# Early fill products, another order in the first conditioning steps, paired sums of squares and a later bias preparation in a decoder block on one core

## The chip, the cores and the metric

The kernel runs on one core of one Trainium2 chip. Its time is that of one execution on the device in microseconds (us); the median of several executions counts. The engines are TensorE (PE, with its weight loads as PEld), VectorE (DVE), ScalarE (ACT), GpSimd (POOL) and SyncE (SP), whose queue issues nearly all loads. TensorE has two clock levels, 1.2 and 2.4 GHz; the profile gives the granted clock as a share of the upper one.

## What is computed

One decoder block on 256 tokens of width 1024: a conditioned norm, one wide input product, a convolution branch and a gated linear recurrence branch (8 heads), their gated merge through three square products, then a mixture of 32 experts of which each token takes four, and a last norm.

```python
mod = silu(c) @ w_ada + b_ada                    # six sections of 1024
sh1, sc1, ga1, sh2, sc2, ga2 = split(mod, 6)
h = rmsnorm(x, g_mix) * (1 + sc1) + sh1
p = h @ w_in                                     # 8 parts of 1024 columns
y_conv = silu(layernorm(conv31(p_a * sigmoid(p_b)))) @ w_conv_out
y_hg   = (rmsnorm_head(hgrn2(p_q, p_f, p_i, lb)) * silu(p_g)) @ w_hgrn_out
x = x + ga1 * ((sigmoid(p_gc) * y_conv + sigmoid(p_gh) * y_hg) @ w_out)
h2 = rmsnorm(x, g_ffn) * (1 + sc2) + sh2
x = x + ga2 * moe(h2)      # top 4 of 32, clamped SwiGLU, w1[e] 1024x2048, w2[e] 1024x1024
out = rmsnorm(x, g_final)
```

## The kernel before, in words

**Slots and loads.** All weights, and the large intermediates, live in 22 slots of 1 MiB. `queue` lists the loads in the order of use, `load` issues the next one on SP's queue, and `free` gives a slot back and calls `pump`, which issues as many loads as the list `LOADS` says for that release: 19 at the start (line 42), then 0 to 3 for each release. From the experts on, `pump` loads whenever a slot is free. Small tiles come from a pool of eight buffers (`temp`), and products go to eight PSUM banks (`bank`).

**Products in two parts.** Weights and activations are split into a rounded part and a rest, both float32r. `split_half(n, i)` (from line 359) does it for half of weight block n: ScalarE casts (line 370), VectorE or GpSimd subtracts (line 372; the lists `SPLIT_DVE` and `SPLIT_HALF` say which). `prod_kt` (line 386) issues three matmuls for each 128 rows and 128 columns, so a block of 1024 by 256 has 48. `block_product(n)` splits block n + 1 while it multiplies block n. Float32 products that aren't split are issued as two MATMUL instructions each.

**First steps.** Lines 228 to 304 and the loop over `st` are in a hand-written order on PE, ACT and DVE. The square of x (line 232) and the sigmoid of c (line 234) come first, then the sum of squares over the rows by `column_parts` and `column_total` (lines 243 to 252), the reciprocal root (lines 225 and 226), and the lower bounds of the recurrence (lines 266 to 271, with an exponential). For each of eight column tiles `mod_first` makes shift and scale (line 285, a copy at 289) and `h_tile` turns and applies them (lines 295 to 304). Between these, the products of the first four input blocks ("early", at the steps `EARLY_AT` = 0, 1, 3, 7) run tile by tile as e_ps.

**Input blocks.** The loop over `IN_ORDER` has 32 blocks. After a block the results are worked on, and steps of other jobs are taken: convolution taps (line 437, VectorE), recurrence levels, `layer_norm` (from block 23), `hgrn_out`, and the four later sections of the modulation, one of 16 loads at each block of `MOD_AT` (5, 7, 8, 11, then 12, 13, 14, 15, then 18, 22, 25, 26, then 27, 28, 30, 31). When a section's four loads are multiplied, the next step copies its sum (line 332) and makes columns or rows of it by further products: lines 336 to 343 for sections 1 and 2, line 348 for section 0, line 353 (bb) for section 3. Here the instructions are put in order by a planner that goes by program order and its own estimates.

**The end of the front.** `hgrn_out` sums the squares of each pair of heads (line 576) one pair after the other. `layer_norm` sums its squares in four groups (lines 546 and 548). Then come the products with w_hgrn_out (four blocks, ho_ps), w_conv_out (co_ps), w_out (wo_ps), the residual (lines 811 to 813), the router and the experts. `prepare` (lines 635 to 644) turns the expert biases into three bfloat16 parts on VectorE; two of its steps are taken after each co_ps block. In the co_ps loop lines 773 to 777 make the merged activations mg in two parts.

Of the kernel before, what the change touches and what calls it, by code (L numbers as in the profile page):

```python
# [41 lines left out]
LOADS = (19, 0, 0, 0, 0, 0, 1, 0, 0, 1, 0, 0, 0, 0, 1, 2, 2, 2, 2, 0, 0, 1, 0, 0, 1, 1, 0, 0, 1, 0, 0, 1, 1, 0, 0, 1, 0, 0, 0, 0, 0, 0, 0, 0, 0, 1, 0, 0, 0, 1, 1, 0, 0, 0, 0, 0, 0, 1, 1, 0, 0, 1, 1, 0, 0, 1, 0, 0, 0, 0, 0, 0, 1, 0, 0, 1, 1, 0, 0, 1, 0, 0, 0, 0, 0, 1, 0, 0, 1, 1, 0, 0, 1, 1, 2, 0, 0, 0, 0, 3, 1, 0, 0, 1, 1, 0, 0, 1, 1, 3, 0, 0, 0, 0, 0, 0, 0, 0, 0, 1, 1, 1, 0, 1, 1, 2, 0, 0, 1, 0, 0, 1, 0, 0, 1, 0, 0, 1, 1, 0, 0, 0, 0, 0, 1, 1, 0, 0, 0, 0, 1, 1, 2, 1, 0, 0, 1, 0, 0, 1, 0)  # L42
# [48 lines left out]
def block_kernel(ctx, tc, xT_d, x_d, prm_d, con_d, wada0_d, wada_d, bada_d, gfin_d, win_d, wco_d, who_d, wo_d,  # L91
# [48 lines left out]
    def free(n=1):  # L140
        live[0] -= n
        pump()
# [88 lines left out]
    xsq = slot([P, KT, T], "xsq")  # L231
    nc.scalar.activation(xsq, xT, AF.Square)
    csig = of_pre(KT)
    nc.scalar.activation(csig, prm[:, PR_C:PR_C + KT], AF.Sigmoid)
    nc.vector.tensor_tensor(out=csig, in0=csig, in1=prm[:, PR_C:PR_C + KT], op=ALU.mult)
    cact = [csig[:, kt:kt + 1].to_broadcast([P, 32]) for kt in range(KT)]
# [18 lines left out]

    ss = column_total(column_parts(xsq, "ss"), "ss")
    free()
    rs = temp("rs")
    rsqrt_mean(rs[:, :T], ss, D)


# [4 lines left out]
    nc.vector.tensor_tensor(out=lbx, in0=lbp[:, 0, :], in1=lbp[:, 1, :], op=ALU.max)  # L266
    nc.vector.tensor_tensor(out=lbe, in0=lbp, in1=lbx.unsqueeze(1).to_broadcast([P, 2, KT]), op=ALU.subtract)
    nc.scalar.activation(lbe, lbe, AF.Exp)
    nc.vector.tensor_tensor(out=lbx, in0=lbe[:, 0, :], in1=lbe[:, 1, :], op=ALU.add)
    nc.vector.reciprocal(out=lbx, in_=lbx)  # L270
    nc.vector.tensor_tensor(out=lbv, in0=lbe, in1=lbx.unsqueeze(1).to_broadcast([P, 2, KT]), op=ALU.mult)
# [8 lines left out]
    def mod_first(kt):  # L280
        w = fetch(("ada0", kt))
        m = bank("mod0")
        for i in range(2):
            for g in range(4):
                nc.tensor.matmul(m[g * 32:(g + 1) * 32, :256], lhsT=cact[2 * g + i], rhs=w[:, 2 * g + i, :],
                                 start=i == 0, stop=i == 1)
        free()
        sb = temp("mod0s")
        nc.scalar.copy(out=sb[:, :256], in_=m[:, :256])
        return sb  # L290

# [19 lines left out]
    ga1 = None  # L311

    def mod_section(j):

        nonlocal ga1
        m = bank(f"mod{j}")
        for k2 in range(4):
            w = fetch(("ada", j, k2))
            if k2 == 0 and j in (0, 3):
                for b in range(2):  # L320
                    nc.tensor.matmul(m[b * 32:(b + 1) * 32, :],
                                     lhsT=ident[:32, 4 + 2 * j + b:5 + 2 * j + b].to_broadcast([32, 32]),
                                     rhs=bada, start=True, stop=False)
            for h in range(2):
                for b in range(2):
                    g = 2 * h + b
                    nc.tensor.matmul(m[g * 32:(g + 1) * 32, :], lhsT=cact[2 * k2 + h],
                                     rhs=w[:, h, b * 512:(b + 1) * 512], start=k2 == 0 and (h == 1 or j in (1, 2)), stop=k2 == 3)
            free()
            yield  # L330
        sb = temp(f"mods{j}")
        nc.scalar.copy(out=sb, in_=m)
        if j in (1, 2):
            mt = bank("mt")
            for kt in range(KT):
                nc.tensor.matmul(mt[:, kt:kt + 1], lhsT=sb[:, (kt % 4) * P:(kt % 4 + 1) * P], rhs=selb[kt // 4],
                                 start=True, stop=True)
            if j == 1:
                nc.vector.tensor_tensor(out=sh2, in0=mt[:, :KT], in1=prm[:, PR_SH2:PR_SH2 + KT], op=ALU.add)
            else:  # L340
                nc.vector.scalar_tensor_tensor(out=g2, in0=mt[:, :KT], scalar=1.0, in1=prm[:, PR_SC2:PR_SC2 + KT],
                                               op0=ALU.add, op1=ALU.add)
                nc.vector.tensor_tensor(out=g2, in0=g2, in1=prm[:, PR_GFFN:PR_GFFN + KT], op=ALU.mult)
        elif j == 0:
            ga1 = [temp("ga1") for _ in range(2)]
            for b in range(2):
                gb = bank("gb")
                nc.tensor.matmul(gb, lhsT=selb[b].to_broadcast([P, P]), rhs=sb, start=True, stop=True)
                nc.scalar.copy(out=ga1[b], in_=gb)
        else:  # L350
            bb = bank("bb")
            for b in range(2):
                nc.tensor.matmul(bb[b * 64:(b + 1) * 64, :], lhsT=selb[b].to_broadcast([P, 64]), rhs=sb,
                                 start=True, stop=True)
            nc.scalar.copy(out=ga2, in_=bb)


    parts = {}

    def split_half(n, i):  # L360

        if n >= len(units):
            return
        key = units[n]
# [169 lines left out]
    def layer_norm():  # L534
# [34 lines left out]
    def hgrn_out():  # L569
# [8 lines left out]
        before = None  # L578
        for hp in range(HEADS // 2):
            if before is not None:  # L580
                square_sums(*before)
# [12 lines left out]
            before = hp, osq  # L594
            yield
        square_sums(*before)
# [53 lines left out]
    early, done = [], []  # L650
    for st in range(KT + 2):
        if st < KT:
            ms = mod_first(st)
        for n in range(N_EARLY):
            if EARLY_AT[n] == st - 1:
                for i in range(2):
                    split_half(n, i)
                early.append(bank("e_ps").rearrange("p (m t) -> p m t", m=2))
                done.append(0)
# [19 lines left out]

    nc.vector.tensor_copy(tri, prm[:, PR_TRI:PR_TRI + P])  # L680
# [69 lines left out]
    step(mods, 100)  # L750

# [16 lines left out]
    for b in range(4):  # L768
        ps = block_product(36 + b, yx, "co_ps", last=b == 3)
        if b % 2 == 0:  # L770
            mg.append(split_slot(f"mg{b // 2}"))
# [8 lines left out]
        step(preps, 2)  # L780
    step(preps, 100)
# [33 lines left out]
    for b in range(3):  # L815
# [5 lines left out]
        for t in range(NT):  # L821
            residual(ps, b, t)

# [593 lines left out]
```

## Time and profile before

| | us |
|---|---|
| median of three runs | 1334.53 |
| lowest and highest | 1331.17, 1335.19 |
| profiled execution | 1334.8 |
| its span, first to last instruction | 1333.1 |
| TensorE busy in the span | 1225.6 (92%) |
| VectorE, ScalarE, GpSimd busy | 547.8, 274.2, 145.4 |
| read from memory | 477.63 MB |

A busy share is a mean over stages that have different limits, and matmuls are pipelined, so TensorE's share doesn't tell that it is the bound. It is read stage by stage: how dense the loads are, which engine is full, and which wait ends last.

### The profile page before, as it was taken

The numbers are of one execution on the slowest core, as the hardware profiler recorded it, in microseconds if no ns is written. First come the engines' busy times: TensorE is split into PE (matmuls) and PEld (weight loads), VectorE is DVE, ScalarE is ACT, GpSimd is POOL, SyncE is SP. The second block draws the span as 40 slices with busy tenths as digits, with TensorE's granted clock in tenths as the row PEclk, the third lists the DMA queues.
The fourth block names the chain that finished last, engine by engine and source line by source line (L and its number), as shares of the span: only waits on it lengthen the run. The fifth ranks groups of instructions, "written<-read, shape, count | busy, mean of one in ns | idle before, by whom it ended". The sixth has DMA issues, their size and how long they took to land. (4 is left out here: it accounts for less than half of the span.)

```text
span 1333.1 us, 18930 instructions
## 1 busy us (share of the span) xinstructions
PE 1225.6 (92%) x7761; PEld 671.4 (50%) x7761; DVE 547.8 (41%) x1065; ACT 274.2 (21%) x434; POOL 145.4 (11%) x63
## 2 busy tenths in 40 slices
PE   5999999999899999999899898888898889999997
PEld 3899877679864343443434333232333324334432
DVE  4498999645844242333223313222223312323322
ACT  4445534653321010101001000000000000000112
POOL 3257535122300000000000000000000000000000
PEclk8999989999999999999999999999899998999999
DMA  9993435646689999999999999999999999989994
GB/s 380 412 394 112 145 128 221 235 174 235 251 314 405 420 420 419 420 420 420 421 419 420 420 420 420 420 421 420 420 420 418 419 421 420 418 347 420 419 419 168
DMA packets 71493, 480.57 MB, mean 360 GB/s; under 512 B 7488, under 2 KB 8768, under 8 KB 16064
## 3 DMA queue, kind: packets, MB, share of 16 engines
q1 hardware_dynamic: 70928, 477.99, 88.0%
q8 instruction: 94, 1.54, 0.5%
q10 hardware_dynamic: 432, 0.72, 0.2%
q14 instruction: 39, 0.32, 0.1%
HBM read 477.63 MB, written 1.05 MB: 359 GB/s over the span
## 5 line engine op out<-in xcount | busy, mean ns | idle before, releaser
L987 PE MATMUL u_gl<-w_w,xg 128*64 128x512 f32 x1024 | 273.5, 599 | 23.5 <-DMA w_w<-in_w_dram 23.4
L987 PE MATMUL u_lin<-w_w,xg 128*64 128x512 f32 x1024 | 272.1, 594 | 0.8 <-issue 0.8
L1026 PE MATMUL yp<-w_w,li 128*64 128x512 f32 x992 | 223.3, 602 | 13.5 <-ACT li L1013 10.2
L994 DVE TENSOR_SCALAR gl<-u_gl 128x512 f32<-128x512 f32 (+1 forms) x33 | 22.3, 675 | 338.9 <-PE u_gl L987 338.9
L987 PEld LDWEIGHTS u_gl<-w_w,xg 128*64 128x64 f32 x1024 | 77.1, 137 | 166.7 <-issue 92.0
L987 PEld LDWEIGHTS u_lin<-w_w,xg 128*64 128x64 f32 x1024 | 81.9, 137 | 139.5 <-issue 139.5
L386 PEld LDWEIGHTS p_ps<-h,ws 128*128 128x128 f32 x1152 | 141.2, 193 | 11.7 <-issue 5.9
L386 PE MATMUL p_ps<-h,ws 128*128 128x256 f32 x1152 | 146.2, 287 | 0.0
L1026 PEld LDWEIGHTS yp<-w_w,li 128*64 128x64 f32 x992 | 69.1, 138 | 149.8 <-issue 128.0
L1036 DVE TENSOR_TENSOR yg<-yp,ga 64x512 f32<-64x512 f32 x60 | 41.3, 689 | 233.0 <-PE yp L1026 232.4
L372 POOL TENSOR_TENSOR ws<-w_in,ws 128x1024 fp32r<-128x1024 f32 x45 | 114.0, 2549 | 121.9 <-ACT ws L370 113.6
L995 ACT ACTIVATE u_gl<-gl 128x512 f32<-128x512 f32 (+1 forms) x33 | 19.4, 589 | 407.8 <-DVE gl L994 407.7
L437 DVE SCALAR_TENSOR_TENSOR cv<-u,pre,cv 128x255 f32<-128x255 f32 (+25 forms) x240 | 95.1, 456 | 9.1 <-ACT cv L434 8.3
L951 PE MATMUL xg_ps<-o,w_x 128*128 128x128 f32 (+1 forms) x544 | 68.6, 286 | 17.4 <-DVE li L996 10.3
L951 PEld LDWEIGHTS xg_ps<-o,w_x 128*128 128x128 f32 x544 | 65.0, 199 | 30.6 <-DVE li L996 21.7
L370 ACT CAST ws<-w_in 128x1024 fp32r<-128x1024 f32 x64 | 65.9, 1046 | 47.9 <-PE p_ps L386 25.0
L1039 ACT ACTIVATE ys0h<-yg,by 64x512 fp32r<-64x512 f32 x30 | 21.6, 720 | 244.0 <-DVE yg L1036 244.0
L955 DVE TENSOR_SCALAR xg<-xg_ps,g,sh 128x128 f32<-128x128 f32 (+1 forms) x136 | 45.4, 395 | 25.0 <-issue 16.6
L1013 ACT COPY li<-ta 128x512 f32<-128x512 f32 (+1 forms) x33 | 18.9, 573 | 120.6 <-PE ta L1010 120.6
L372 DVE TENSOR_TENSOR ws<-w_in,ws 128x1024 fp32r<-128x1024 f32 x19 | 25.0, 1331 | 14.0 <-ACT ws L370 14.0
L386 PE MATMUL wo_ps<-ws,mg 128*128 128x256 f32 x192 | 26.2, 297 | 3.5 <-ACT ws L370 1.8
L1040 DVE SCALAR_TENSOR_TENSOR ys0l<-yg,by,ys0h 64x512 fp32r<-64x512 f32 x30 | 22.4, 748 | 12.8 <-ACT ys0h L1039 11.9
(286 smaller groups left out, 1111.3 us busy)
## 6 DMA issues: line engine op xcount, KB each, us to landing
w_w<-in_w_dram SPq DMA_DIRECT2D x383, 1024.0 KB, 19.9
w_in<-in_win_dram SPq DMA_DIRECT2D x32, 1024.0 KB, 12.2
w_ada<-in_wada_dram SPq DMA_DIRECT2D x24, 1024.0 KB, 16.1
w_ho<-in_who_dram SPq DMA_DIRECT2D x4, 1024.0 KB, 4.7
w_co<-in_wco_dram SPq DMA_DIRECT2D x4, 1024.0 KB, 5.1
w_wo<-in_wo_dram SPq DMA_DIRECT2D x4, 1024.0 KB, 8.3
xT<-in_xT_dram SPq DMA_DIRECT2D x1, 1024.0 KB, 7.2
w_x<-in_x_dram SPq DMA_DIRECT2D x1, 1024.0 KB, 6.5
```

Of the source, the lines that this page charges most:

```text
L370: nc.scalar.copy(out=to[:, 0], in_=w[:, ks, :])
L372: (nc.vector if dve else nc.gpsimd).tensor_tensor(out=to[:, 1], in0=w[:, ks, :], in1=to[:, 0].bitcast(F32), op=ALU.subtract)
L386: nc.tensor.matmul(out, lhsT=lt, rhs=rh, start=first and kt == 0 and i == 0, stop=kt == KT - 1 and i == 2, skip_group_check=not first)
L437: nc.vector.scalar_tensor_tensor(out=cv[:, ct, s:], in0=u[i][:, m, :T - s], scalar=tap, in1=cv[:, ct, s:], op0=ALU.mult, op1=ALU.add)
L951: nc.tensor.matmul(ps[:, i, cs], lhsT=x2[:, t, kt * P:(kt + 1) * P], rhs=o[:, 0, t, cs], start=t == 0, stop=t == NT - 1)
L955: nc.vector.tensor_scalar(out=xg[h][:, i, cs], in0=ps[:, i, cs], scalar1=g2[:, kt:kt + 1], scalar2=sh2[:, kt:kt + 1], op0=ALU.mult, op1=AL ...
L987: nc.tensor.matmul(up[nb][g * 64:(g + 1) * 64, :], lhsT=xg[kt // 4][:, kt % 4, i * CAP:(i + 1) * CAP], rhs=w[:, c:c + 512], start=False, s ...
L994: nc.vector.tensor_scalar(out=gl[:, c], in0=up[0][:, c], scalar1=LIMIT, scalar2=None, op0=ALU.min)
L1026: nc.tensor.matmul(yp[g * 64:(g + 1) * 64, :], lhsT=aT[:, kt % 4, kt // 4, :], rhs=w[:, kk, g * 512:(g + 1) * 512], start=False, stop=kt = ...
L1036: nc.vector.tensor_tensor(out=y[rows, :], in0=yp[gs, :], in1=ga2[gs, :], op=ALU.mult)
L1039: nc.scalar.activation(hi[rows, :], y[rows, :], AF.Copy, scale=by[rows, :])
L1040: nc.vector.scalar_tensor_tensor(out=lo[rows, :], in0=y[rows, :], scalar=by[rows, :], in1=hi[rows, :].bitcast(F32), op0=ALU.mult, op1=ALU. ...
```

## The change

It changes seven places.

1. In the first steps the sigmoid comes ahead of the square, and 24 fill products of a constant tile by itself (128 by 128, float32, into a bank that nobody reads) are issued on TensorE ahead of the sum of squares. `mod_first(0)` comes between the partial sums and their total. After the steps 0 to 3 there are 6, 6, 3 and 3 more fills.
2. The lower bounds become a function that is called behind the hand-written order.
3. The first input block is split before the loop, not in its step 1; one of the first 19 loads is issued two releases later instead.
4. The columns and rows of a modulation section become a function in the list `late`, which is emptied behind the next block's product (behind the last section, at once).
5. The variance's groups are taken in pairs, with the two groups' products alternating; each group writes its own 32 partitions.
6. The four sums of squares of the head pairs are issued together, behind the last pair.
7. The first half of the first w_out block is split one block earlier, and the steps of the bias preparation are taken in the w_out loop.

```diff
-LOADS = (19, 0, 0, 0, 0, 0, 1, ...
+LOADS = (18, 0, 0, 1, 0, 0, 1, ...
...
-    xsq = slot([P, KT, T], "xsq")
-    nc.scalar.activation(xsq, xT, AF.Square)
     csig = of_pre(KT)
     nc.scalar.activation(csig, prm[:, PR_C:PR_C + KT], AF.Sigmoid)
     nc.vector.tensor_tensor(out=csig, in0=csig, in1=prm[:, PR_C:PR_C + KT], op=ALU.mult)
+    xsq = slot([P, KT, T], "xsq")
+    nc.scalar.activation(xsq, xT, AF.Square)
+    idle = bank("idle")[:, 0:P]
+    def fill(n):
+        for _ in range(n):
+            nc.tensor.matmul(idle, lhsT=ones, rhs=ones, start=True, stop=True)
+    fill(24)
...
-    ss = column_total(column_parts(xsq, "ss"), "ss")
-    free()
-    rs = temp("rs")
-    rsqrt_mean(rs[:, :T], ss, D)
...
+    def lower_bounds():
...
+    ss = column_parts(xsq, "ss")
+    ms0 = mod_first(0)
+    ss = column_total(ss, "ss")
+    free()
+    rs = temp("rs")
+    rsqrt_mean(rs[:, :T], ss, D)
...
+    late = []
     def mod_section(j):
...
         nc.scalar.copy(out=sb, in_=m)
-        if j in (1, 2):
...
+        def rows():
+            nonlocal ga1
+            if j in (1, 2):
...
+        late.append(rows)
...
-        for g in range(4):
-            sq = temp("csq").rearrange("p (i t) -> p i t", i=2)
-            nc.scalar.activation(sq, cv[:, 2 * g:2 * g + 2, :], AF.Square)
+        for gs in ((0, 1), (2, 3)):
+            sqs = [temp("csq").rearrange("p (i t) -> p i t", i=2) for _ in gs]
+            for g, sq in zip(gs, sqs):
+                nc.scalar.activation(sq, cv[:, 2 * g:2 * g + 2, :], AF.Square)
             for i in range(2):
-                nc.tensor.matmul(part[g * 32:(g + 1) * 32, :T], lhsT=ones[:, 0:32], rhs=sq[:, i, :],
-                                 start=i == 0, stop=i == 1)
+                for g, sq in zip(gs, sqs):
+                    nc.tensor.matmul(part[g * 32:(g + 1) * 32, :T], lhsT=ones[:, 0:32], rhs=sq[:, i, :],
+                                     start=i == 0, stop=i == 1)
...
-            if before is not None:
-                square_sums(*before)
...
-            before = hp, osq
+            before.append((hp, osq))
             yield
-        square_sums(*before)
+        for b in before:
+            square_sums(*b)
...
+    for i in range(2):
+        split_half(0, i)
     for st in range(KT + 2):
         if st < KT:
-            ms = mod_first(st)
+            ms = mod_first(st) if st else ms0
...
+        if st < 4:
+            fill((6, 6, 3, 3)[st])
...
     order.__exit__(None, None, None)
+    lower_bounds()
...
         ps = early[n] if n < N_EARLY else block_product(n, hx, "p_ps", part == 4, n == 31)
+        while late:
+            late.pop(0)()
...
     step(mods, 100)
+    while late:
+        late.pop(0)()
...
         ps = block_product(36 + b, yx, "co_ps", last=b == 3)
+        if b == 2:
+            split_half(40, 0)
...
-        step(preps, 2)
-    step(preps, 100)
     x2 = fetch(("x",))
...
             residual(ps, b, t)
+        step(preps, 2)
+    step(preps, 100)
```

## Rows read from the trace of the kernel before

**Rows 1.** The page's rate of the loads in 40 equal slices of the span.
```profile
GB/s 380 412 394 112 145 128 221 235 174 235 251 314 405 420 420 419 420 420 420 421 419 420 420 420 420 420 421 420 420 420 418 419 421 420 418 347 420 419 419 168
```

**Rows 2.** Waits, 800 to 950 us: engine, line, releaser: us in total, times, longest.
```profile
PEld u_gl L987 <- DMA w_w<-in_w_dram: 38.8, 29, 2.1
```

**Rows 3.** Windows of 4 us: busy PE, PEld, DVE, ACT, POOL (instructions), clock, DMA share, GB/s.
```profile
412.00:416.00 4.00, 4.00 (x24) 1.30 (x22) 0.06 (x1) 0.00 (x0) 0.00 (x0) 1.00 0.86 291
```

**Rows 4.** Waits of SP's queue, 340 to 400 us, the largest.
```profile
SPq L123 <- PE wo_ps L386: 19.6, 5, 6.9
```

**Rows 5.** Timeline to 60 us (start, duration, idle before), and one PE window with clock.
```profile
10.03 1.93 PE L243 MATMUL ssp<-xsq,pre 128*32 128x256 f32 x16 [10.03 <-ACT xsq L232]
14.23 1.75 DVE L226 RECIPROCAL rs<-rs 128x256 f32<-128x256 f32 x1 [2.52 <-ACT rs L225]
17.31 1.07 PE L285 MATMUL mod<-w_ada,pre 128*32 128x256 f32 x16
17.74 0.48 DVE L300 SCALAR_TENSOR_TENSOR xT<-xT,pre,rs 128x256 f32<-128x256 f32 x1
20.05 9.89 POOL L372 TENSOR_TENSOR ws<-w_in,ws 128x1024 fp32r<-128x1024 f32 x4 [19.49 <-ACT ws L370]
20.30 2.38 DVE L300 SCALAR_TENSOR_TENSOR xT<-xT,pre,rs 128x256 f32<-128x256 f32 x1
20.54 1.93 PE L285 MATMUL mod<-w_ada,pre 128*32 128x256 f32 x16 [0.59 <-DMA w_ada<-in_wada_dram]
...
34.00 0.50 PE L295 MATMUL mt<-con,mod0s 128*128 128x1 f32 x4
...
48.42 11.75 PE L386 MATMUL e_ps<-h,ws 128*128 128x256 f32 x96
...
16.00:18.00 2.00, 1.22 (x19) 1.00 1.03 430
24.00:26.00 2.00, 2.00 (x21) 0.50 1.04 434
```

**Rows 6.** A 20 us window of the taps, and the wait for the last tap.
```profile
120.00:140.00 20.00, 19.76 (x267) 16.89 (x267) 20.00 (x37) 9.16 (x13) 12.83 (x5) 0.91 0.59 201
...
230.19 0.40 PE L243 MATMUL mup<-cv,pre 128*32 128x256 f32 x1 [0.54 <-DVE cv L437]
```

**Rows 7.** Timeline, TensorE, 226 to 273 us.
```profile
226.12 1.05 PE L576 MATMUL oss<-osq,pre 128*32 128x512 f32 x2
...
245.31 1.05 PE L548 MATMUL varp<-csq,pre 128*32 128x256 f32 x4
...
262.24 1.08 PE L353 MATMUL bb<-mods,con 128*64 128x512 f32 x4 [2.19 <-ACT mods L332]
...
272.88 1.06 PE L327 MATMUL mod<-w_ada,pre 128*32 128x512 f32 x8
```

**Rows 8.** Timeline at the first w_out block, VectorE's groups 328 to 349 us, one window.
```profile
330.23 0.68 DVE L774 TENSOR_TENSOR tm<-tm,gates 128x512 f32<-128x512 f32 x1
...
348.49 0.38 PE L386 MATMUL wo_ps<-ws,mg 128*128 128x256 f32 x1 [1.81 <-ACT ws L370]
...
350.01 6.19 PE L386 MATMUL wo_ps<-ws,mg 128*128 128x256 f32 x37 [1.14 <-DVE ws L372]
...
351.73 2.15 DVE L774 TENSOR_TENSOR tm<-tm,gates 128x512 f32<-128x512 f32 x1
...
356.75 7.21 PE L386 MATMUL wo_ps<-ws,mg 128*128 128x256 f32 x58 [0.55 <-DVE mg L777]
...
L640 DVE COPY b<-b 32x1024 bf16<-32x1024 bf16 x9 | 3.7, 416 | 0.1
L635 DVE CAST b<-w_b 96x1024 bf16<-96x1024 f32 x3 | 3.6, 1216 | 0.0
L637 DVE TENSOR_TENSOR w_b<-w_b,b 96x1024 f32<-96x1024 f32 x2 | 2.4, 1212 | 0.0
...
360.00:380.00 20.00, 20.00 (x172) 19.92 (x170) 9.46 (x16) 10.58 (x26) 2.56 (x2) 1.00 0.70 251
```

More of the change, by code (lines that the diff above doesn't have):

```diff
@@ L41 @@
 MOD_EXTRA = {}
-LOADS = (19, 0, 0, 0, 0, 0, 1, 0, 0, 1, 0, 0, 0, 0, 1, 2, 2, 2, 2, 0, 0, 1, 0, 0, 1, 1, 0, 0, 1, 0, 0, 1, 1, 0, 0, 1, 0, 0, 0, 0, 0, 0, 0, 0, 0, 1, 0, 0, 0, 1, 1, 0, 0, 0, 0, 0, 0, 1, 1, 0, 0, 1, 1, 0, 0, 1, 0, 0, 0, 0, 0, 0, 1, 0, 0, 1, 1, 0, 0, 1, 0, 0, 0, 0, 0, 1, 0, 0, 1, 1, 0, 0, 1, 1, 2, 0, 0, 0, 0, 3, 1, 0, 0, 1, 1, 0, 0, 1, 1, 3, 0, 0, 0, 0, 0, 0, 0, 0, 0, 1, 1, 1, 0, 1, 1, 2, 0, 0, 1, 0, 0, 1, 0, 0, 1, 0, 0, 1, 1, 0, 0, 0, 0, 0, 1, 1, 0, 0, 0, 0, 1, 1, 2, 1, 0, 0, 1, 0, 0, 1, 0)
+LOADS = (18, 0, 0, 1, 0, 0, 1, 0, 0, 1, 0, 0, 0, 0, 1, 2, 2, 2, 2, 0, 0, 1, 0, 0, 1, 1, 0, 0, 1, 0, 0, 1, 1, 0, 0, 1, 0, 0, 0, 0, 0, 0, 0, 0, 0, 1, 0, 0, 0, 1, 1, 0, 0, 0, 0, 0, 0, 1, 1, 0, 0, 1, 1, 0, 0, 1, 0, 0, 0, 0, 0, 0, 1, 0, 0, 1, 1, 0, 0, 1, 0, 0, 0, 0, 0, 1, 0, 0, 1, 1, 0, 0, 1, 1, 2, 0, 0, 0, 0, 3, 1, 0, 0, 1, 1, 0, 0, 1, 1, 3, 0, 0, 0, 0, 0, 0, 0, 0, 0, 1, 1, 1, 0, 1, 1, 2, 0, 0, 1, 0, 0, 1, 0, 0, 1, 0, 0, 1, 1, 0, 0, 0, 0, 0, 1, 1, 0, 0, 0, 0, 1, 1, 2, 1, 0, 0, 1, 0, 0, 1, 0)
 TAPS = (1, 0, 0, 0, 5, 4, 10, 6, 5, 5, 13, 6, 16, 14, 17, 11, 5, 8, 0, 6, 0, 0, 0, 0, 0, 3, 13, 9, 17, 15, 9, 5)
@@ L265, in block_kernel @@
     lbv = of_pre(2 * KT).rearrange("p (l k) -> p l k", l=2)
[L266 to L271, printed above, removed]
+    def lower_bounds():
+        nc.vector.tensor_tensor(out=lbx, in0=lbp[:, 0, :], in1=lbp[:, 1, :], op=ALU.max)
+        nc.vector.tensor_tensor(out=lbe, in0=lbp, in1=lbx.unsqueeze(1).to_broadcast([P, 2, KT]), op=ALU.subtract)
+        nc.scalar.activation(lbe, lbe, AF.Exp)
+        nc.vector.tensor_tensor(out=lbx, in0=lbe[:, 0, :], in1=lbe[:, 1, :], op=ALU.add)
+        nc.vector.reciprocal(out=lbx, in_=lbx)
+        nc.vector.tensor_tensor(out=lbv, in0=lbe, in1=lbx.unsqueeze(1).to_broadcast([P, 2, KT]), op=ALU.mult)
     sc1b = of_pre(KT)
@@ L311, in block_kernel @@
     ga1 = None
+    late = []
     def mod_section(j):
-        nonlocal ga1
         m = bank(f"mod{j}")
@@ L332, in mod_section @@
         nc.scalar.copy(out=sb, in_=m)
-        if j in (1, 2):
[L334 to L339, printed above, removed]
-            else:
[L341 to L355, printed above, removed]
@@ new lines, in rows @@
+        def rows():
+            nonlocal ga1
+            if j in (1, 2):
+                mt = bank("mt")
+                for kt in range(KT):
+                    nc.tensor.matmul(mt[:, kt:kt + 1], lhsT=sb[:, (kt % 4) * P:(kt % 4 + 1) * P], rhs=selb[kt // 4],
+                                     start=True, stop=True)
+                if j == 1:
+                    nc.vector.tensor_tensor(out=sh2, in0=mt[:, :KT], in1=prm[:, PR_SH2:PR_SH2 + KT], op=ALU.add)
+                else:
+                    nc.vector.scalar_tensor_tensor(out=g2, in0=mt[:, :KT], scalar=1.0, in1=prm[:, PR_SC2:PR_SC2 + KT],
+                                                   op0=ALU.add, op1=ALU.add)
+                    nc.vector.tensor_tensor(out=g2, in0=g2, in1=prm[:, PR_GFFN:PR_GFFN + KT], op=ALU.mult)
+            elif j == 0:
+                ga1 = [temp("ga1") for _ in range(2)]
+                for b in range(2):
+                    gb = bank("gb")
+                    nc.tensor.matmul(gb, lhsT=selb[b].to_broadcast([P, P]), rhs=sb, start=True, stop=True)
+                    nc.scalar.copy(out=ga1[b], in_=gb)
+            else:
+                bb = bank("bb")
+                for b in range(2):
+                    nc.tensor.matmul(bb[b * 64:(b + 1) * 64, :], lhsT=selb[b].to_broadcast([P, 64]), rhs=sb,
+                                     start=True, stop=True)
+                nc.scalar.copy(out=ga2, in_=bb)
@@ L358, in block_kernel @@
+        late.append(rows)
     parts = {}
+    split = set()
     def split_half(n, i):
-        if n >= len(units):
+        if n >= len(units) or (n, i) in split:
             return
+        split.add((n, i))
         key = units[n]
@@ L576, in square_sums @@
             nc.tensor.matmul(oss[hp * 32:(hp + 1) * 32, :], lhsT=ones[:, 0:32], rhs=osq, start=True, stop=True)
-        before = None
+        before = []
         for hp in range(HEADS // 2):
-            if before is not None:
-                square_sums(*before)
             ob = bank("ob").rearrange("p (m t) -> p m t", m=2)
@@ L656, in block_kernel @@
                 for i in range(2):
-                    split_half(n, i)
+                    if n:
+                        split_half(n, i)
                 early.append(bank("e_ps").rearrange("p (m t) -> p m t", m=2))
```

## The prediction

> **What bounds the kernel now.** I read the page's rate line first [rows 1]. In its 33 us slices the loads move 380 to 412 GB/s for the first 100 us, then 112 to 314, and from about 400 us some 420 to the end, with one dip to 347. So there are two regimes. In the long second one, the experts, transfers set the pace: TensorE waits for expert weights there [rows 2]. The finest windows show where that stream last runs dry: 0.86 busy at 412 to 416 us [rows 3]; the later dip, some 750 us on, stands behind a conditional expert and moves with the rest. What keeps it from filling earlier is in the waits of SP's queue between 340 and 400 us: the largest is for TensorE's w_out products [rows 4]. The 22 slots are full, and each load waits until TensorE has used a slot. So the stream starts when TensorE arrives, and what TensorE gains before some 400 us should move the whole rest, by as much. That is the lever of this change, which touches nothing behind it.
>
> Before 400 us TensorE is busy nearly throughout, but not always the bound. Until 34 us it follows a chain of small steps through ScalarE, VectorE and GpSimd, partly at the lower clock [rows 5]. From 48 us it streams: 96 products in 11.75 us, 122 ns each [rows 5]. Then VectorE fills up: 20.00 of 20 us busy in a typical stretch of the convolution taps, and at 230 us TensorE sits waiting for the last tap [rows 6]. So a gain on TensorE alone between 110 and 230 us is paid back in that wait; a shift of the start survives, because VectorE's full stretch begins with what TensorE hands it.
>
> **The first steps.** The change issues 24 fills, sigmoid ahead of the square, the first modulation product between the two halves of the sum of squares, and takes the lower bounds out. Today the sum's 16 matmuls take 1.93 us at 10.03, against 1.07 for a modulation's 16 of the same form at 17.31 [rows 5]. The clock column reads 1.00 until 18 us, but 1.93 is the duration of 1.2 GHz, so I go by it. At full clock this group is 0.9 us shorter. But the square root must still follow a table load and the copies, and the reciprocal at 14.23 us barely moves (estimate: 14.4). What moves is the step behind it: xT is scaled at 17.74 us, though the reciprocal is over at 15.98; without the exponential in between that can be 1.5 us earlier. Later steps gain where the clock was low: 0.50 at 24 to 26 us, and the third modulation's 1.93 at 20.54 against 1.07 [rows 5]. The ceiling comes from the loads: the third modulation waited for its weights until 20.54; the fifth comes three loads of 1 MiB later, at 420 GB/s 2.5 us each, 28 us; with 1.07 for the product and half a microsecond for the copy its transposes can start at 29.6 us, against 34.00 now. So the start gains between 0 and 4.4 us. I take **2.5**, because the block-0 subtraction on GpSimd is moved into these steps too (first rival).
>
> The fills have no row of their own. Nearest are the variance's four float32 instructions, 1.05 us for 256 columns each [rows 7]. A fill is two such instructions of 128 columns, so as an estimate 0.26 us at full clock and twice that at half. The first 24 take 6 to 12 us of time in which TensorE waits for the square, which ends at 10.03 [rows 5]; the other 18 take 5 to 9 us, beside waits for the copies. On the path: 0 to 2 us. Without that cover they would cost all of it. The lower bounds return behind the hand-ordered part; their results are first needed beyond 100 us, so 0, at most a table load and a half on ScalarE. Of the loads, one moves from the first batch to behind block 0's split; the queue is then 18 loads deep, so 0.
>
> **Rows of the modulation sections.** Deferring them takes a copy's latency off TensorE's queue. Sections 1 and 2 lie before 230 us: 0 by the argument above. Section 3 is the one with a price: TensorE waits 2.19 us before bb [rows 7]. The next section's products fill that time. Section 0 is popped right after it is made, so nothing changes. I take all of it, **2.2**; the lower bound is 1.0, if the products that come forward wait for the same ScalarE work.
>
> **Sums of squares.** Each of the four head-pair sums takes 1.05 us alone, while eight matmul instructions of the same width, spread over the four column groups, take 1.06 [rows 7]. All four together thus save 3.1. One of them, at 226.12, is ahead of the wait at 230 and doesn't count: **2.0**, between 1.0 and 3.1. In the variance the last group of four instructions takes 1.05 us; four such groups after each other would take 4.2, two pairs 2.1. The first two groups already overlap partly, so **1.6**, between 1.0 and 2.1. The squares now hold their buffers longer, four of the eight; I count 7 or 8 in use at the worst place, so no wait.
>
> **Between w_conv_out and w_out.** The first w_out block should take 48 times 122 ns, 5.9 us. It starts when the product before ends (348.49 less its idle 1.81, 346.68) and ends at 357.97 (ten of the 58 products issued from 356.75 are its last): 11.3 us. The difference, 5.4, is waits: 1.81 for ScalarE's first cast of w_out, 1.14 for VectorE's rest of it, 0.55 for mg, and a slow stretch between (37 products in 6.19 us, 167 ns each) [rows 8]. The early half split removes the first two. The bias preparation, 3.6 + 2.4 + 3.7 = 9.7 us of VectorE [rows 8], leaves the queue ahead of mg, so the last mg can be ready by about 350 us; TensorE needs it after 36 products, at 351.1. A GpSimd subtraction beside it can stretch two of its steps, as 2.15 us shows for one that takes 0.68 otherwise (the difference, 1.5, twice). So **4.2**, between 2.3 and 5.4.
>
> The 9.7 us of VectorE now lie between the w_out products. From 360 to 380 us it is busy 9.46 of 20 [rows 8], so 10.5 are free: 0, but up to 3 if they come ahead of a split that TensorE waits for. The raw bias slot is also freed three blocks later. By the tail of the load plan (1, 1, 2, 1, 0, 0, 1, 0, 0, 1, 0 from that release on) each of seven loads then waits one release longer, some 3 us, in a stretch that moves forward by more than that: 0. For all costs together I take **-0.5**.
>
> **Sum.** 2.5 + 2.2 + 2.0 + 1.6 + 4.2 - 0.5 = 12.0 us. The profiled execution took 1334.8 us, its span and 1.7 around it, and lies 0.3 above the median of the runs. 1334.5 - 12.0 = **1322.5 us**. A measurement of this kernel can tell about 0.3%, 4 us, from no change.
>
> **The rivals.** *The start gives nothing.* The GpSimd subtraction of block 0 starts at 20.05 us now and will start some 4 us after the square. Beside it the scaling of an h tile takes 2.38 us, alone 0.48 [rows 5]: 1.9 more. Two tiles, the first and its remainder, meet it: 3.8, more than the 2.5. Then 9.5 us remain: 1325. For it: the two rows. Against it: the same subtractions already stand in the chain, only a tile later. The Trainium skill, page "SBUF — State Buffer", section "Who interferes with whom", says that a VectorE instruction with two SBUF inputs and a GpSimd one that reads SBUF exclude each other for a whole instruction; by that rule this rival holds whenever the two meet, and the trace's 2.38 beside 0.48 agrees.
>
> *The loads set the expert stream.* If its start is not given by TensorE's releases but by the order of the loads, the gain vanishes: 1334.5 less 0 to 4, say 1333. For it: the stream is dense again from 416 us on, and seven loads are put off. Against it: the 19.6 us that SP waited for w_out products [rows 4].
>
> *Slower: the preparation lands on the path.* VectorE, between two w_out products, must give the residual, the split and now 3.2 us of preparation, against 6 us of TensorE for one block. If it comes ahead of the split in the queue, or GpSimd blocks its two subtractions, all 9.7 and two blocks of 1.5 to 1.9 go onto the path, and the 4.2 are not gained: 12.0 - 4.2 - 13.2 = -5.4, so 1340. It decides as soon as VectorE's work in a block exceeds TensorE's. Against it: 10.5 us free.
>
> *All terms at their upper ends*: 4.4 + 2.2 + 3.1 + 2.1 + 5.4 = 17.2, 1317.3.
>
> **How the numbers follow.** The forecast, 8 to 16 us off, 0.57; nothing from the start 0.12; upper ends 0.11; the loads 0.13; slower 0.07. The first three are faster by more than 0.3%: 0.80; same 0.13; slower 0.07. The forecast's own range is 1318.5 to 1326.5; to hold 8 in 10 it has to take in the upper ends in part and the first rival whole, and the lower sums of the terms: 1315 to 1331.
>
> **What would show it.** The 96 products of the early blocks should start 2 to 3 us before 48.4; bb should have no wait in front; one group of eight oss instructions should take about 1.1 us; the first w_out block should take 6 to 8 us; the router should start about 12 us earlier, and the dense stream with it. I am wrong if TensorE still waits for the last tap at 230 us, if the wait for mg only moves to a later block, or if TensorE is early at 390 us and the loads are not.

## The result, and the profile after

The changed kernel takes **1348.13 us** (median of 4 runs, 1345.47 to 1349.87), against 1333.89 of the kernel before (4 runs): a ratio of 1.0095, 95% interval 1.0068 to 1.0122. It is slower, by 14 us, where 12 us less were forecast. Its profiled execution, the slowest of the four, has a span of 1348.2 us against 1333.1.

Where the two part is read from the timeline: for each block of 48 products, and for the first bias product of each expert, the time at which it starts. Block 2 is the one that started at 48.42 us before [rows 5]; the blocks are numbered in the order in which TensorE runs them.

| stretch (us) | before | after | difference |
|---|---|---|---|
| start to block 2 (first steps) | 48.42 | 48.29 | -0.13 |
| block 2 to 25 (input blocks, taps, to the mean of the layer norm) | 183.53 | 184.88 | +1.35 |
| block 25 to 27 (variance, oss) | 21.03 | 22.28 | +1.25 |
| block 27 to 36 (bb, ho) | 70.00 | 67.94 | -2.06 |
| block 36 to expert 0 (co, w_out, router) | 65.52 | 66.69 | +1.17 |
| **start of expert 0** | 388.50 | 390.07 | **+1.57** |
| start of expert 9 | 626.08 | 627.65 | +1.57 |
| start of expert 26 | 1163.48 | 1164.13 | +0.65 |
| expert 26 to 27 | 25.40 | 33.13 | +7.73 |
| expert 27 to 28 | 27.59 | 34.30 | +6.71 |
| expert 28 to the end | 116.65 | 116.63 | -0.02 |

So there are two results: a front that gained nothing, and 14.4 us lost in two experts out of 32, 800 us behind the last edited line.

The page's rate line of after answers to [rows 1]: nearly the same to slice 34, then 378, 368, 388, 389 where before had 418, 347, 420, 419.

```profile
GB/s 383 411 381 134 119 127 219 251 189 196 281 313 407 422 420 420 420 419 421 420 420 421 419 420 420 421 421 420 420 420 418 419 421 421 378 368 388 389 413 89
```

The rate falls, but the loads are not what TensorE waits for most. The waits of TensorE from 1110 us to the end (engine, line, releaser: us in total, times, longest us) begin like this in after; before has no line with "issue" in this stretch, its largest is 2.0.

```profile
PE xg_ps L983 <- issue: 3.9, 1, 3.9
PE yp L1058 <- issue: 3.5, 1, 3.5
PE u_gl L1019 <- DMA w_w<-in_w_dram: 2.7, 5, 0.6
```

"issue" is time in which an engine waited for nothing that the profile shows. In the timeline (start, duration, operation, idle before) both stand in the middle of a run of products, between two with the same operands:

```profile
1184.43 1.50 PE L1058 MATMUL yp<-w_w,li 128*64 128x512 f32 x5 [0.34 <-ACT li L1045]
1189.45 5.94 PE L1058 MATMUL yp<-w_w,li 128*64 128x512 f32 x20 [3.52 <-issue]
...
1212.40 1.16 PE L983 MATMUL xg_ps<-o,w_x 128*128 128x128 f32 x8 [0.78 <-DVE li L1028]
1217.44 5.28 PE L983 MATMUL xg_ps<-o,w_x 128*128 128x128 f32 x24 [3.88 <-issue]
```

What arrives then is code. In the queues' part of the page (queue, packets, MB, share) the queue q8 carries instructions, 16.4 KB in each packet; the two lines behind it are its packets at 1187 to 1188 and at 1214 to 1216 us, each some 2 us ahead of the end of a stop.

```profile
q8 instruction: 95, 1.56, 0.5%
...
q8 instruction: 1, 0.02, 6.0%
...
q8 instruction: 1, 0.02, 3.2%
```

It is so everywhere: the traces of all fourteen kernels of this document have 42 such stops behind the start of expert 0, and in each stop exactly one packet of q8, of 16,384 bytes, starts 2.2 to 2.6 us ahead of its end.

After each stop TensorE runs at its lower level. The windows show it (columns as in [rows 3]; the clock is the third number from the end, a mean of the window, 1.00 being 2.4 GHz and 0.50 being 1.2):

```profile
1190.00:1193.00 3.00, 3.00 (x10) 0.83 (x8) 0.00 (x0) 0.00 (x0) 0.00 (x0) 0.60 0.99 415
1218.00:1224.00 6.00, 5.98 (x31) 5.56 (x29) 2.55 (x8) 0.32 (x1) 0.00 (x0) 0.57 1.02 421
```

That is how 3.5 and 3.9 us of idle time become more. Not all of the 7.7 us of expert 26 is the stop's, though: TensorE enters that expert at the lower clock, some 20 us ahead of the stop.

```profile
1161.00:1169.00 8.00, 8.00 (x21) 2.42 (x21) 0.00 (x0) 0.00 (x0) 0.00 (x0) 0.57 1.02 423
```

So it does in the kernel with 64 dummies below, which has no stop there (0.51 at 1159.5 to 1165.5 us): without a stop the stretch from expert 26 to 27 takes 25.40 to 27.89 us in twelve kernels, the next one 27.6 in all. Counted from the end of that slow entry, expert 26 takes 5.6 us more in after than in before, so that the two stops cost 5.6 and 6.7 us.

Before has such stops too, at 643, 941 and 1095 us, two in xg_ps and one in yp. The waits of TensorE in before from 500 us to the end have these two lines with "issue" that are over 1 us (idle us in total, times, longest):

```profile
PE xg_ps L951 <- issue: 7.0, 2, 3.5
PE yp L1026 <- issue: 3.2, 1, 3.2
```

Up to expert 25 TensorE waits for weights [rows 2], and there the stops are absorbed: from expert 9 to 26 the fourteen kernels take 533.5 to 537.9 us, whether two or three stops lie in that stretch (none has fewer). From expert 26 on it hardly waits for weights (1.2 us in all in before), and before has no stop there.

In the front, the rows of after that answer to [rows 5 to 7] (the two DVE rows are the scalings of the first h tile):

```profile
9.95 1.07 PE L251 MATMUL ssp<-xsq,pre 128*32 128x256 f32 x16 [1.55 <-ACT xsq L235]
...
16.07 1.69 DVE L312 SCALAR_TENSOR_TENSOR xT<-xT,pre,rs 128x256 f32<-128x256 f32 x1
18.41 1.84 DVE L316 SCALAR_TENSOR_TENSOR h<-xT,pre,h 128x256 fp32r<-128x256 f32 x1 [0.64 <-ACT h L315]
...
19.56 2.91 PE L241 MATMUL idle<-pre 128*128 128x128 f32 x12
22.40 1.94 PE L289 MATMUL mod<-w_ada,pre 128*32 128x256 f32 x16
...
229.81 0.64 PE L251 MATMUL mup<-cv,pre 128*32 128x256 f32 x1 [2.29 <-DVE cv L456]
...
242.86 0.62 PE L569 MATMUL varp<-csq,pre 128*32 128x256 f32 x2 [2.24 <-ACT csq L566]
243.41 0.55 PE L405 MATMUL p_ps<-h,ws 128*128 128x256 f32 x1
243.88 1.92 PE L569 MATMUL varp<-csq,pre 128*32 128x256 f32 x6
...
261.47 1.07 PE L597 MATMUL oss<-osq,pre 128*32 128x512 f32 x8
...
270.38 1.08 PE L368 MATMUL bb<-mods,con 128*64 128x512 f32 x4
```

The sum of squares takes 1.07 us and the scaling of xT starts 1.7 us earlier, as expected; the third modulation stands behind 2.91 us of fills. The wait for the last tap is there, and larger. The oss group takes 1.07 us for all eight and bb waits for nothing, as expected; but varp now waits 2.24 us, and its products run at 1.2 GHz behind the wait (1.92 us for six; at full clock six take 1.05).

At w_out, the rows of TensorE, then of VectorE, then one of GpSimd, that answer to [rows 8], and a window (columns as in [rows 3]):

```profile
346.51 4.72 PE L405 MATMUL wo_ps<-ws,mg 128*128 128x256 f32 x38
352.67 7.21 PE L405 MATMUL wo_ps<-ws,mg 128*128 128x256 f32 x58 [1.44 <-DVE mg L809]
...
366.36 1.87 PE L834 MATMUL lg<-wr,x2T 128*128 128x32 f32 x16
370.94 1.46 PE L824 MATMUL tp<-con,w_x 128*128 128x128 f32 x4 [2.71 <-DVE w_x L842]
372.05 6.91 PE L405 MATMUL wo_ps<-ws,mg 128*128 128x256 f32 x39
...
363.30 2.91 DVE L655 CAST b<-w_b 96x1024 bf16<-96x1024 f32 x1
366.24 1.22 DVE L657 TENSOR_TENSOR w_b<-w_b,b 96x1024 f32<-96x1024 f32 x1
367.47 1.28 DVE L660 COPY b<-b 32x1024 bf16<-32x1024 bf16 x3
368.78 1.23 DVE L391 TENSOR_TENSOR ws<-w_wo,ws 128x1024 fp32r<-128x1024 f32 x1
369.92 0.42 DVE L841 TENSOR_TENSOR tmo<-wo_ps,ga 128x256 f32<-128x256 f32 x1
...
363.21 2.44 POOL L391 TENSOR_TENSOR ws<-w_wo,ws 128x1024 fp32r<-128x1024 f32 x1 [11.14 <-ACT ws L389]
...
360.10:372.10 12.00, 9.15 (x75) 8.71 (x73) 11.24 (x17) 5.96 (x15) 2.44 (x1) 0.90 0.62 229
```

The same 39 products in before:

```profile
372.53 4.92 PE L386 MATMUL wo_ps<-ws,mg 128*128 128x256 f32 x39
```

The first block is 4.1 us early at its end (353.96 against 358.04). Then the transposes of the router wait for the residual, which stands in VectorE's queue behind 5.4 us of preparation and a split; the cast of 2.91 us has GpSimd's subtraction beside it, and VectorE is busy 11.24 of these 12 us. Behind the wait TensorE runs at the lower clock: the last 39 products of w_out take 6.91 us, where before takes 4.92. The wait and the clock together take all 4.1 back by expert 0.

The waits of SP's queue from 340 to 400 us, which answer to [rows 4], show the same from the loads' side: less is waited for w_out's products (before 19.6), and more for VectorE's part of the splits (14.0 us, before 7.0).

```profile
SPq L123 <- DVE ws L391: 14.0, 3, 5.7
SPq L123 <- PE wo_ps L405: 12.7, 4, 6.4
```

### The profile page after: what moved, and what is told of

Its sections match the earlier page's. It is cut to its first block, busy times and chain, and to the rows that moved or that the text cites. A ratio compares the mean times of both kernels' runs of the same rounds, so it can differ in the third digit from the quotient of the medians.

```text
span 1348.2 us, 19103 instructions
## 1 busy us (share of the span) xinstructions
PE 1234.7 (92%) x7845; PEld 679.0 (50%) x7845; DVE 547.4 (41%) x1065; ACT 272.7 (20%) x433; POOL 144.7 (11%) x63
## 3 DMA queue, kind: packets, MB, share of 16 engines
HBM read 477.63 MB, written 1.05 MB: 355 GB/s over the span
## 5 line engine op out<-in xcount | busy, mean ns | idle before, releaser
L456 DVE SCALAR_TENSOR_TENSOR cv<-u,pre,cv 128x229 f32<-128x229 f32 (+28 forms) x240 | 95.3, 460 | 8.6 <-ACT cv L453 7.8
```

The source lines that it names most:

```text
L456: nc.vector.scalar_tensor_tensor(out=cv[:, ct, s:], in0=u[i][:, m, :T - s], scalar=tap, in1=cv[:, ct, s:], op0=ALU.mult, op1=ALU.add)
```

## The experiments

The first question was the tail. **Theory A**: it is TensorE's code. The 42 fills and one wait more make its program 169 instructions longer ahead of all that follows (the trace has 84 weight loads and 84 products for the 42 fills, four instructions each), so that everything behind lies elsewhere in the blocks in which code is brought. The Trainium skill, page "Runtime: NRT & Kernel Launch", section "Instruction fetch mechanics", gives 256 instructions for a 16 KiB block and says that a taken branch whose target is not among the blocks at hand makes the engine wait; the packets here have that size, and nearly every expert has two conditional branches (58 in the trace of before). **Theory B**: the tail follows from the rearranged front.

**The kernel before, with 42 small dummy products at the front.** TensorE is idle there until 10 us.

```
+    idle = bank("idle")
+    for _ in range(42):
+        nc.tensor.matmul(idle[0:32, 0:32], lhsT=ones[:, 0:32], rhs=ones[:, 0:32], start=True, stop=True)
     cact = [csig[:, kt:kt + 1].to_broadcast([P, 32]) for kt in range(KT)]
```

> The kernel before with 42 small dummy float32 products (32x32) at the very front, where TensorE is idle until 10 us; nothing else is changed. They make TensorE's program 168 instructions longer ahead of all that follows, as the fills of the change do (169). Theory A (the loss sits in TensorE's code: everything behind the fills lies elsewhere in the 256-instruction blocks in which queue q8 brings code, and two code stalls come to lie behind expert 25): 1344 to 1349 us, with stops of about 4 us of TensorE, each beside a 16,384-byte packet of q8, behind 1165 us. Theory B (the loss comes from the rearranged front: the load plan, the preparation in the w_out blocks, later slots): 1332 to 1336 us, no stop that before has not.

Measured: 1345.15 us, ratio 1.0086 (1.0061 to 1.0111). None of the change's other edits is in it, and it loses 11.4 us of the change's 14.2. Its timeline has the same two stops, in the same two experts (the second at 1212.60):

```profile
1180.02 1.50 PE L1034 MATMUL yp<-w_w,li 128*64 128x512 f32 x5 [0.34 <-ACT li L1021]
1184.35 4.45 PE L1034 MATMUL yp<-w_w,li 128*64 128x512 f32 x12 [2.82 <-issue]
```

Experts 26 and 27 take 5.2 and 5.7 us more than before's; this kernel enters expert 26 at full clock. Theory A holds, B doesn't.

**The same with 64 dummies**, 256 instructions.

> The kernel before with 64 of the same small dummy products at the front: 256 instructions, one whole code block, so that every later instruction keeps its place within its block. Theory A: 1332 to 1336 us, the stops of TensorE where before has them (about 643, 941, 1095 us). Theory B: the same time, 1332 to 1336. If merely more instructions or a longer program cost the time, this one should lose more than the one with 42.

Measured: 1334.51 us, ratio 1.0009 (0.9990 to 1.0028): no difference, with more added than above. Its waits of TensorE from 500 us on have one line with "issue" that is over 1 us, and these stops lie at 642 and 941 us:

```profile
PE xg_ps L959 <- issue: 7.0, 2, 3.6
```

The one at 1095 us is missing, so the place within a block is not the whole rule.

**The changed kernel without its fills.** The two calls of fill are taken out.

```
-    fill(24)
-        if st < 4:
-            fill((6, 6, 3, 3)[st])
```

> The changed kernel without any of its 42 fill products; the rest of the change stays. TensorE's program is then 4 instructions longer than before's (waits). Theory A: the tail is that of before, and the time is before's plus what the front lost (1.6 us at expert 0, give or take what the fills give): 1332 to 1338 us, no pair of stops at 1185 and 1213. Theory B: the tail stays as in the changed kernel, 1345 to 1350.

Measured: 1331.23 us, ratio 0.9990 (0.9973 to 1.0008). The stops are at 643, 942 and 1095 us, where before has them; expert 0 starts at 388.70. That is theory A, with a time a little below its range.

**The changed kernel with all its fills and 22 small dummies more**, 257 instructions in all.

> The changed kernel with all its fills and 22 small dummy products more at the front: 169 + 88 = 257 instructions more than before, one whole code block and one. Theory A: the stops of TensorE go back to where before has them and the time is before's plus 0 to 3 us: 1332 to 1338 us. Theory B: the work is that of the changed kernel plus some microseconds of TensorE at a place where it is idle: 1346 to 1350.

Measured: 1332.01 us, ratio 0.9991 (0.9972 to 1.0011). The waits of TensorE from 1110 us to the end now begin as before's do, with no "issue":

```profile
PE yp L1064 <- ACT li L1051: 2.0, 6, 0.3
PE arm_ps L1103 <- DVE arm L1098: 1.9, 1, 1.9
```

More work than in the changed kernel, and 16 us less time. With that the tail is settled, as far as its cause goes: the count of instructions ahead of it. The counts tried (0 to 5, 168, 169, 256 and 257 more than before) don't tell a period of 256 from one of 128 or 64. What remains of the change can't be told from nothing: the intervals of both kernels without the two stops hold 1.

The second question was where the front's forecast gain went. All further kernels are built on the changed kernel without fills, or on before, and their tails show no stop behind expert 26.

**The preparation back in the co_ps loop.**

```
         if b % 2 == 1:
             free()
+        step(preps, 2)
+    step(preps, 100)
...
         for t in range(NT):
             residual(ps, b, t)
-        step(preps, 2)
-    step(preps, 100)
```

> The changed kernel without its fills (as in the run of that kernel, expert 0 at 388.7 us), with the bias preparation put back from the w_out blocks into the co_ps blocks; the early split of the first w_out half stays. Theory C (the preparation's copies and subtractions stand on VectorE ahead of the residuals, so that the transposes of the router wait 3.3 us and expert 0 another 1.9): the wait of tp falls under 1 us, block 43 starts 5 us ahead of before's and expert 0 at 383.5 to 385.5 us; the time 1326 to 1330 us. Theory D (the 5.2 us won by block 42 come from the preparation having left the co_ps blocks, not from the early split): block 41 starts where before has it, expert 0 at 387 to 389 us, the time 1330 to 1333.

Measured: 1333.78 us, ratio 0.9997 (0.9978 to 1.0016), block 36 to expert 0 in 68.51 us. Theory C is half right: the wait of tp falls to 0.6, but wo_ps now waits 3.3 us for VectorE's part of the split and 1.9 for mg, and the stretch is longer, not shorter. Of theory D, block 41 starts where before has it (358.15 us, before 358.04), and expert 0, at 389.95, misses its range by a microsecond.

**The sums of squares of the heads one pair behind, as before.**

```
-        before = []
+        before = None
         for hp in range(HEADS // 2):
+            if before is not None:
+                square_sums(*before)
...
-            before.append((hp, osq))
+            before = hp, osq
...
-        for b in before:
-            square_sums(*b)
+        square_sums(*before)
```

> The changed kernel without its fills, with the sums of squares of the o heads (oss) issued one head pair behind again, as before; the rest of the change stays. Theory E (the oss products, put off to the end, no longer cover the squares that varp waits for, so that what oss wins comes back as the 3.4 us wait of varp): the wait of varp falls under 1 us, some 1 to 3 us of waits come back at oss, and the block behind (28) starts 0 to 2 us earlier than 263.3 us; the time 1328 to 1332 us. Theory F (varp's wait is the pairing of its own squares and has nothing to do with oss): varp waits 3 us or more as before this edit, block 28 at 264 to 266 us; the time 1331 to 1334.

Measured: 1327.98 us, ratio 0.9959 (0.9941 to 0.9977). varp waits no longer, and block 25 to 27 takes 20.84 us. The same stretch takes 22.2 to 26.2 us in the four kernels that issue oss at the end; the longest is the one without fills:

```profile
238.88 1.06 PE L568 MATMUL varp<-csq,pre 128*32 128x256 f32 x2 [3.43 <-ACT csq L565]
239.87 0.58 PE L404 MATMUL p_ps<-h,ws 128*128 128x256 f32 x1
240.38 1.92 PE L568 MATMUL varp<-csq,pre 128*32 128x256 f32 x6
```

Theory E holds in the main: the oss products had filled the time until the squares were there. They were not alone: with oss one pair behind, six instructions of a modulation section stand in the same place (1.06 us), and with oss at the end the planner puts these ahead of block 25.

**Both put back.**

> The changed kernel without its fills, with both put back: the preparation in the co_ps blocks, oss one pair behind. Theories C and E: expert 0 at 382 to 385 us and the time 1324 to 1329 us. Theories D and F: expert 0 at 387 to 390, the time 1331 to 1334. If the stretch from expert 10 to 25, which runs at the pace of the loads, swallows what the front wins, expert 0 is early and the time is still 1330 to 1333.

Measured: 1330.95 us, ratio 0.9983 (0.9968 to 0.9999); expert 0 at 387.89, block 36 to expert 0 in 67.96 us. The oss part repeats (20.84), the early half without the moved preparation costs again. Both numbers are, to 0.1 us, those of D and F, though F is out by the oss part; C's gain is out.

**The kernel before with the order of the first steps alone.** The whole of the edit between csig and h_tile, the split of unit 0 up front, and the lower bounds behind.

> The kernel before with the other order of its first steps alone (loads, csig ahead of the square, first mod product ahead of the total, lower bounds behind the early blocks, first unit's halves split at once), without any fill. The block of 48 at 48.42 us starts at 46.2 to 46.6 us, as in the changed kernel without fills. If the front passes it on, expert 0 starts at 386.3 to 387 us and the time is 1331 to 1332; if a later wait of the front (lv for k, varp) swallows it, expert 0 starts at 388 to 389 and the time is 1332.5 to 1334.5.

Measured: 1331.27 us, ratio 0.9980 (0.9962 to 0.9997); block 2 at 46.45, expert 0 at 388.27. The time fits the first reading, the start of expert 0 the second. The front swallowed the 2.0 us: 1.6 us are lost between block 27 and 36 (71.57 instead of 70.00; the kernel with 42 dummies has 71.56 there). Nine kernels with this order and without fills start block 2 between 46.35 and 48.97 us, three with the old order between 46.85 and 48.42. No gain of the first steps is shown. The nine have the same instructions there, so single executions of them differ by up to 2.6 us, and a gain of 2.5 can't be told from that. The clock is where two of them part: at 28.5 us of the changed kernel without fills (block 2 at 46.36) twelve early products take 1.67 us, at 29.2 us of the kernel with block 2 at 48.86 they take 2.91.

The last four runs build on the kernel of 1327.98 us (the expectations call it the best so far) and take the w_out edit apart.

**Without the w_out edit** (the preparation in the co_ps loop, no early half).

> The best kernel so far (the change without fills and with oss one pair behind) without the whole w_out edit: the preparation in the co_ps blocks, no early half of the first w_out unit. The stretch from the start of the last co_ps block to expert 0, which was 47.74 us in the kernel before, 48.61 in the best kernel so far and 50.17 with the early half alone, comes to 47.5 to 48.0 us if the w_out edit as a whole costs time (theory G), and the time is 1326.5 to 1330 us. If the 49.1 us of the change were due to where its front stood in time (theory H), it stays at 48.4 or more.

Measured: 1327.05 us, ratio 0.9946 (0.9925 to 0.9967); last co_ps block to expert 0 in 47.72 us, as before's. Theory G holds, H doesn't.

**The preparation spread over both loops**, with the early half.

```
+        if b < 3:
+            step(preps, 1)          # co_ps loop
...
-        step(preps, 2)
+        step(preps, 1)              # w_out loop
```

> The best kernel so far with the steps of the preparation spread: one behind each of the first three co_ps blocks, one behind each w_out block; the early half stays. Theory G, in detail: each place has room for some of it, the wait of tp falls from 3.7 to under 1.5 us and block 41 keeps its early start; last co_ps block to expert 0: 45.5 to 47.5 us, time 1324 to 1328. Rival: VectorE is full in both places, and the wait only moves between wo_ps and tp: 48 to 50 us, time 1328 to 1332.

Measured: 1329.85 us, ratio 0.9967 (0.9950 to 0.9985); 50.62 us. The rival holds, with a stretch above even its range: tp waits 1.9 us in all, but wo_ps waits 3.7 us for mg.

**Without the early half**, the preparation in the w_out loop.

```
-        if b == 2:
-            split_half(40, 0)
```

> The best kernel so far without the early half of the first w_out unit; the preparation stays in the w_out blocks. If the early half has a worth of its own once the preparation is gone from the co_ps blocks, as the prediction had it, the stretch from the last co_ps block to expert 0 grows from 48.6 to 50 to 52 us and the time to 1329 to 1333. If the preparation's place does it all, the stretch stays at 48 to 49 us, the time within 1 us of the best so far.

Measured: **1326.73 us**, ratio 0.9940 (0.9918 to 0.9962), the lowest median; 48.38 us. The second reading holds for the stretch; the time is 1.3 us below the best so far, and the intervals of the two overlap. Its tail has the full clock and TensorE busy 48.06 of 50 us:

```profile
1200.00:1250.00 50.00, 48.06 (x232) 19.19 (x230) 14.29 (x31) 5.25 (x8) 0.00 (x0) 1.00 1.01 420
```

After has 44.17 us busy at a clock of 0.93 in the same window.

**Spread, without the early half.**

> The best kernel so far with the preparation spread (one step behind each of three co_ps blocks, the rest in the w_out blocks) and without the early half. With theory G the stretch from the last co_ps block to expert 0 lies between before's 47.7 and the spread one with the early half: 46.5 to 48.5 us, time 1326 to 1329. If it is longer than the spread kernel's by over 1 us, the early half is worth that much by itself.

Measured: 1328.81 us, ratio 0.9957 (0.9937 to 0.9977); 49.40 us, longer than expected, and shorter than with the early half.

Four of the kernels make a square, by block 36 to expert 0 in us (before: 65.52):

| | preparation in the co_ps loop | in the w_out loop |
|---|---|---|
| no early half | 65.52 | 65.75 |
| early half | 67.96 | 65.97 |

Neither edit gains anything here, alone or together. The two lowest medians are 1326.73 and 1327.05 us; the intervals of all kernels with oss put back lie below 1, and those of these two overlap, so which is better is open. Both leave out the fills and the delayed oss, and keep the deferred rows, the pairs of the variance and the order of the first steps. They are 8 us below before, but expert 0 starts only 3.4 and 4.5 us earlier in their traces; where the rest comes from is not shown.

## Why the prediction was wrong

**"That is the lever of this change, which touches nothing behind it"**: this step failed, and 13.5 of the 15.1 us between the spans lie behind it (15.07 less 1.57 at expert 0), 12.3 of them in the two stops. The fills were priced by the time they take on an idle engine. Their other effect, that they move the whole program behind them within its code blocks, is in no row of a timeline of before. The sign could not be had from the rows. That there was a risk could: the "issue" gaps at 643, 941 and 1095 us stand in the trace of before, each 3.2 to 3.6 us in the middle of a run, and the waits for weights that absorb them there end at expert 25. Which branch meets which end of a block was not worked out: the runs show the dependence on the count, not its rule.

**What the front gains moves the rest.** This held as far as the scatter lets one see. From expert 0 to the end the twelve kernels without stops in the tail take 940.8 to 946.7 us, for starts of expert 0 between 384.0 and 390.0; the scatter is as wide as the starts. The medians agree: 1326.7 to 1329.9 us for the five kernels that start expert 0 at 384.0 to 385.4, 1331.0 to 1334.5 for the seven that start it at 387.7 to 390.0.

**The first steps, 2.5.** The runs show 0.1, and no gain in other kernels with the same order. The product of the squares did fall to 1.07 us. The failed number is the cost of the fills on the path, 0 to 2, for which the sum took at most 0.5. Six of them, 2.91 us at the lower clock, stand ahead of the third modulation, which starts 1.9 us later than in [rows 5]; the clock gives this back by 34 us (1.00 from 28 to 34 us, before 0.72). The first rival's stretching is in the trace as well, but only moved: beside GpSimd's subtraction the scalings of the first tile take 1.69 and 1.84 us (0.48 each before), and those of the second take 0.48 each (2.38 and 1.95 before).

**Rows of the modulation, 2.2.** The stretch from block 27 to 36 falls by 2.06 us. This term was right, and so was its mechanism: bb has no wait.

**oss, 2.0, and varp, 1.6.** The durations were right (1.07 us for the group). The pairs of the variance gave 0.2 us (21.03 to 20.84). The delayed oss cost 1.4 to 5.4 us, because a wait took the place of the products that I removed. Part of this is only moved, by the modulation's instructions that went ahead of block 25; from the start to block 27 the four kernels with oss at the end take 253.4 to 255.4 us, the six with it put back 248.9 to 252.0. I asked that question for the wait at 230 us and not for the next one, twelve microseconds on. The wait at 230 us grew as well (2.29 us), and with it block 2 to 25, by 1.35. The delayed oss isn't its cause, as the wait is 2.0 us with both edits put back, too. In kernels of the same order there that stretch takes 181.7 to 184.9 us; what decides is open.

**w_out, 4.2, with costs of 0.5.** The mechanism was right up to block 42, the first block takes 7.5 us, and TensorE is 4.1 us early there. But "from 360 to 380 us VectorE has 10.5 us free: 0" failed. A mean over 20 us says nothing on the place: the preparation came ahead of the last split and the residual, with one cast that takes 2.91 us beside GpSimd where others take 0.68. That is the rival "the preparation lands on the path", at a smaller price: the stretch is 1.2 us longer instead of 3.7 shorter, where the rival put 13.2 us on the path. By the square, the waits of [rows 8] can be made shorter without a gain. In the traces the place of the preparation takes the gain back: in the w_out loop as the wait of tp and the lower clock behind it, in the co_ps loop, with the early half, as 5.1 us of waits of wo_ps for VectorE's split and for mg. No run puts the preparation at a place where VectorE is free, so whether the 65.5 us can fall is open.

**The sum.** Of 12.0 us the front delivered -1.6: 0.1 for 2.5, 2.1 for 2.2, -2.6 (stretches block 2 to 25 and 25 to 27) for 3.6, -1.2 for 3.7. The tail took 13.5. Without the fills' shift, the same edits make 1332 us, which is within 0.3% of before and one microsecond outside the range.

## What to carry to other kernels

An instruction on an idle engine need not be free: it moves all the code behind it, and here that cost 11.4 us. Before a change is judged, look in the trace for "issue" gaps in the middle of a run and, if they moved, run the change again with its instruction count filled up to the old place in the code blocks. And where products are taken out of a queue, ask for the next wait on it, too; a mean of free time over a window doesn't say whether it is free at the place where it is needed.

## What the runs showed of the hardware

A stop of TensorE for its own code takes 3.3 to 4.2 us from product to product, while the transfers of data go on (a DMA share of 1.03 at 1185 to 1190 us, 1.01 at 1213 to 1218). Its cost is larger than the stop, because the granted clock is at its lower level behind it: 5.2 to 6.7 us in an expert that doesn't wait for weights. 168 added instructions moved the stops from 643, 941 and 1095 us to 700, 1003, 1181 and 1208; 256 and 257 left them where they were, or took one away.

Beside a subtraction on GpSimd a cast on VectorE took 2.91 us instead of 0.68, and a scaling 1.69 to 2.38 instead of 0.48.
